# Both halves of the split activations side by side in one matmul: latents, attention gate and the first output projection of a two-layer trunk

## The chip, the cores and the metric

The kernel runs on one core of one Trainium2 chip. The core has a matrix engine (PE, TensorE, with a separate row PEld for its weight loads), a vector engine (DVE), a scalar engine (ACT) and an engine that issues transfers (SP). They work side by side and wait for each other by semaphores; each runs its own instructions in the order in which the program lists them. The metric is the device time of one execution in microseconds (us), smaller being better. A matmul's sums land in PSUM, a small memory in banks of 512 fp32 columns per partition, from which DVE and ACT read them.

## What is computed

Two layers over 256 tokens of width 2048, in float32. Cut to what matters here:

```python
def hybrid_layer(x, c_act, ...):
    mod = c_act @ w_mod + b_mod
    shift, scale, gate = jnp.split(mod, 3, axis=-1)
    h = rms_norm(x, g_norm) * (1.0 + scale[:, None, :]) + shift[:, None, :]
    proj = h @ w_in
    rq, rk, rv, rg, cq, ckv, kr, mg, bg = jnp.split(proj, points, axis=-1)
    ...                                            # retention branch: o_ret
    y_ret = (o_ret * jax.nn.silu(rg)) @ w_ret_proj
    q = (rms_norm(cq, g_cq) @ w_uq).reshape(B, S, MLA_HEADS, MLA_NOPE + MLA_ROPE)
    ...                                            # rotary part of q and of the shared key
    kv = (rms_norm(ckv, g_ckv) @ w_ukv).reshape(B, S, MLA_HEADS, MLA_NOPE + MLA_DV)
    o_mla = mla_attention(q_nope, q_rope, k_nope, k_rope, v)
    y_mla = (o_mla * jax.nn.silu(mg)) @ w_mla_proj
    g_a, g_b = jnp.split(jax.nn.sigmoid(bg), 2, axis=-1)
    merged = g_a * y_ret + g_b * y_mla
    return x + gate[:, None, :] * (merged @ w_out)
```

`cq` and `ckv` (512 columns each) are the latents, `mg` (2048 columns, 128 for each of 16 heads) is the attention gate, `w_out` is the output projection.

## The kernel before, in words

**Split products.** Every large product is made of three fp32r matmuls. A float32 weight block of 1024 columns per partition is loaded by SP into a buffer `wst` (5 of them), ACT copies its rounded upper part, DVE subtracts to get the rest (`split_into`, L239 to L241), both into one buffer `whl` (3 of them, so a split waits until PE is done with the block three before it). Activations are kept split in the same way by the class `Pairs`: one tile of 1024 columns holds, for two blocks of 128 rows of the contraction, the upper parts (256 tokens each) and behind them the lower parts. A product is upper x upper + upper x lower + lower x upper.

**Which operand moves.** In `proj` (L283) the weights are the stationary operand and the 256 tokens move, so every matmul has 256 columns. `chunk` (L267) lists for one weight block first the two products of the upper weights, one after the other (L273), and then the one of the lower weights (L276); all three add into the same 256 columns of PSUM. Two output blocks of 128 rows share one tile `acc` of 512 columns. In `proj_tok` the activations are stationary and 512 columns of weights move.

**PSUM.** There are four tiles `acc` and four tiles `aux`. A new `acc` tile takes the buffer that comes free first in the order that the scheduler plans, and the first matmul into it waits for the last reader of its predecessor.

**Order.** The kernel is written as one long program; the Tile framework's scheduler plans it with a timeline and writes the order of each engine's instructions. `tc.high_priority()` lets some go ahead of what stands before them. So a change in a few lines can move instructions elsewhere.

**Places that the change touches.** `latent` (L657) makes the normalised latents of a layer by one `proj` of 512 columns (two `acc` tiles), squares and a row norm. The attention loop (L792) goes over 8 pairs of heads in each layer. One turn: products with `w_uq` into two `acc` tiles (`acc<-c,whl`: `a1`, whose readers are ACT's copy `qn` L818 and the split `q1`, and `a2`, whose reader is the rotation, four short DVE products L481 and one L482); products with `w_ukv` into two more (`a1` read by ACT's copy `kn` L836 and the split `k1`, `a2` by ACT's copy `vv` L838); scores (L846 on), softmax; the gate's product (`acc<-h,whl`, four weight blocks) into one `acc` tile, Silu (L873); transposes of the weights of attention (L880) and their copies `p` and `pT` (L882); the product with v (`aux<-p,v`, and `aux<-mg,vv` L887, which reads `pT`); times the gate (L889, DVE); split into `z`. PE works on one turn's gate while the next turn's `w_uq` and `w_ukv` products are close behind. Layer 0's output projection (L915) goes through 16 blocks of `w_out` and adds each, scaled, to `xT` (L921). Layer 1's output projection is another function and stays.

Of the kernel before, what the change touches and what calls it, by code (L numbers as in the profile page):

```python
# [13 lines left out]
AF = mybir.ActivationFunctionType  # L14
ALU = mybir.AluOpType
AX = mybir.AxisListType

P = 128
S = 256
D = 2048  # L20
KT = D // P
# [6 lines left out]
RANK = 512  # L28
# [10 lines left out]
C_MG = C_KR + ROPE  # L39
# [69 lines left out]
def trunk(ctx: ExitStack, tc: tile.TileContext, x, c, positions, w_mod, b_mod, g_norm, w_in, g_cq,  # L109
# [14 lines left out]
    def acc_tile():  # L124
        return pacc.tile([P, 2, S], F32, name="acc", tag="acc")
# [4 lines left out]
    def tmp_tile():  # L130
        return tp.tile([P, 512], F32, name="tmp", tag="tmp")
# [15 lines left out]
    class Pairs:  # L147
# [13 lines left out]
        def block(self, kt, cols=slice(None)):  # L161
            return [u[:, kt % 2, cols] for u in self.pair(kt // 2)]

    cst = cp.tile([P, K_COLS], F32, name="cst")
    DMA.dma_start(cst, consts)
    ident = cst[:, K_ID : K_ID + P]
# [34 lines left out]
    xT = cp.tile([P, KT, S], F32, name="xT")  # L201
# [47 lines left out]
    def load_split(src, nk, n, early=False):  # L249
        if prepared and not early:  # L250
            return prepared.pop(0)
        bg()
        w = load(src, nk, n)
        t = hp.tile([P, 2, 1024], F32R, name="whl", tag="whl")
        hi = t[:, 0, : nk * n].rearrange("p (k n) -> p k n", k=nk)
        lo = t[:, 1, : nk * n].rearrange("p (k n) -> p k n", k=nk)
        with tc.high_priority(offset=SPLITS):
            last_split.append(split_into(hi, lo, w))
        return hi, lo
# [18 lines left out]
    def proj_chunk(accs, hi, lo, k0, nk, span, act):  # L278

        chunk([(accs[j // 2][:, j % 2, :], (hi[:, k, j * P : (j + 1) * P], lo[:, k, j * P : (j + 1) * P]),  # L280
                act.block(k0 + k), k0 + k == span[0] and j % 2 == 0, k0 + k == span[1] - 1, False)
               for k in range(nk) for j in range(hi.shape[2] // P)])

    def proj(w, col, n, act, span=(0, KT)):
        accs = [acc_tile() for _ in range((n + 2 * P - 1) // (2 * P))]
        nk = 1024 // n
        for k0 in range(*span, nk):
            hi, lo = load_split(w[k0 * P : (k0 + nk) * P, col : col + n], nk, n)
            proj_chunk(accs, hi, lo, k0, nk, span, act)
        return accs  # L290

    def proj_tok(w, col, act, span=(0, KT)):
# [163 lines left out]
    def add_squares(sq, pair):  # L456

        src = xT[:, 2 * pair : 2 * pair + 2, :]
        if pair in (0, KT // 2 - 1):
            sq.append(dp.tile([P, 2, S], F32, name="sq", tag="dtab"))  # L460
            A.activation(sq[-1], src, AF.Square)
        else:
            t = tmp_tile().rearrange("p (a b) -> p a b", a=2)
            A.activation(t, src, AF.Square)
            V.tensor_tensor(sq[0], sq[0], t, ALU.add)
# [158 lines left out]
    def layer(l, r, u):  # L624
# [31 lines left out]

        def latent(col, g):  # L657
            dst = Pairs("c")
            accs = proj(W, col, RANK, hh)
            raw = tmp_tile(), tmp_tile()  # L660
            s2 = tmp_tile()
            t = tmp_tile()
            with tc.high_priority():
                for a in range(2):
                    fa = accs[a].rearrange("p a b -> p (a b)")
                    A.activation(raw[a], fa, AF.Copy)
                    A.activation((s2, t)[a], fa, AF.Square)
                V.tensor_tensor(s2, s2, t, ALU.add)
                rr = rstd_rows([s2.rearrange("p (a b) -> p a b", a=2)], RANK)
                for k in range(4):  # L670
                    rk_ = raw[k // 2][:, (k % 2) * S : (k % 2 + 1) * S]
                    V.scalar_tensor_tensor(rk_, rk_, g[:, k : k + 1], rr, ALU.mult, ALU.mult)
                for a in range(2):
                    split_into(*dst.flat(a), raw[a])
            return dst
# [112 lines left out]
        for g in range(MH // 2):  # L788
# [80 lines left out]
            p1 = two(t1, 0, S), two(t1, 512, S)  # L869
            t1 = quarter("v1", F32R)  # L870
            v1 = t1[:, 0:256], t1[:, 256:512]
            accs = proj(W, C_MG + g * 256, 256, hh)
            A.activation(mg, accs[0], AF.Silu)  # L873

            split_into(*v1, vv[:, 0, :])
            po = aux_tile()
# [35 lines left out]
            last_output(w_out[l], mm)  # L912
            return None, None
        sq = []
        for f0, nf in ((0, 4), (4, 4), (8, 4), (12, 2), (14, 2)):  # L915
            accs = proj(w_out[l], f0 * P, nf * P, mm)
            with tc.high_priority() if f0 == 14 else nullcontext():
                for a, acc in enumerate(accs):
                    for b in range(2):
                        f = f0 + 2 * a + b  # L920
                        V.scalar_tensor_tensor(xT[:, f, :], acc[:, b, :], mods[l][:, 32 + f : 33 + f], xT[:, f, :],  # L921
                                               ALU.mult, ALU.add)
                    add_squares(sq, f0 // 2 + a)
                if f0 == 0:
                    A.activation(small(1), sq[0][:, 0, 0:1], AF.Sqrt)
                if f0 == 14:
                    r = spread(rstd_cols(sq, D), dp.tile([P, S], F32, name="r1", tag="dtab"))
            if f0 == 8:
                left(0)
                n = GROUPS[l + 1][0][1]  # L930
                make_amul(l + 1, 0, n)
                u = scaled(l + 1, n)
# [96 lines left out]
```

## Time and profile before

| | |
|---|---|
| median of 3 runs | 2056.74 us (2056.7 to 2057.08) |
| the profiled execution, its own time | 2057.32 us |
| its span from first to last instruction | 2055.5 us |
| PE busy | 2025.8 us, 99%, 12414 recorded matmuls |
| DVE, ACT busy | 1483.6 us (72%), 1061.7 us (52%) |
| DMA | 460.59 MB, 224 GB/s over the span |
| granted clock of PE | 0.997 of full speed |

Busy time of PE counts a matmul until its result is out; matmuls overlap, so the distance from the start of one group to the start of the next is the better measure of what they cost. A timeline row gives the start, the time until the end, engine, line, operation, output and inputs (buffer numbers left out; the moving input is named first), partitions x columns and, as x16, how many instructions were merged; in square brackets the engine's idle time before it and what ended it. An fp32 matmul of `aux<-mg,vv` or `aux<-qkn` is recorded twice, an fp32r one once.

### The profile page before, as it was taken

To read this page: it belongs to the slowest core of one execution; us is meant where nothing else is said; L and a number is where in the kernel's file an instruction comes from. 1 tells how busy PE (TensorE), PEld (TensorE's weight loads), DVE (VectorE), ACT (ScalarE), POOL (GpSimd) and SP (SyncE) were. 2 spreads that over 40 slices of the span, in tenths; PEclk is the share of its full clock that TensorE was granted. 3 is DMA by queue.
4 is the path that set the end of the run, shared out by engine and by line. 5 is a ranking of instruction groups with operands and counts; after the bars stand their busy time and mean duration, and the time that the engine had idled before them with its cause. 6 is when DMAs were issued, how large, how long until landed. Compare 5 with 4: busy or idle time off the path is not lost.

```text
span 2055.5 us, 31773 instructions
## 1 busy us (share of the span) xinstructions
PE 2025.8 (99%) x12414; PEld 1802.8 (88%) x12414; DVE 1483.6 (72%) x2082; ACT 1061.7 (52%) x1489; POOL 0.2 (0%) x4
## 2 busy tenths in 40 slices
PE   7999999999999999999999999999999999999998
PEld 4888888998899998889998888889889999988887
DVE  5799986778777777775577776568776877765574
ACT  4554355654456664444454464456544666644453
POOL 0000000000000000000000000000000000000000
PEclk9999999999999999999999999999999999999999
DMA  8998966567866668875569966665677666666572
GB/s 315 321 310 274 308 198 194 159 191 259 302 191 195 195 187 274 281 267 185 182 196 333 326 209 189 194 180 156 198 238 223 205 185 195 208 224 192 190 243 90
DMA packets 251222, 460.59 MB, mean 224 GB/s; under 512 B 18464, under 2 KB 68032, under 8 KB 251072
## 3 DMA queue, kind: packets, MB, share of 16 engines
q1 hardware_dynamic: 251072, 458.57, 69.8%
q8 instruction: 97, 1.59, 0.3%
q14 instruction: 53, 0.43, 0.1%
HBM read 456.41 MB, written 2.10 MB: 223 GB/s over the span
## 4 chain that ended last, share of the span: by engine, by line
PE 94%; DMA 3%; DVE 2%; ACT 1%; issue 1%; SPq 0%; ACTq 0%; DVEq 0%
PE acc L273 57%; PE acc L276 28%; DMA ring<-in_w_mod 2%; DMA wmod<-in_w_mod 1%; PE aux L264 1%; PE aux L265 1%; PE aux L263 1%; PE acc L263 1%; PE acc L264 1%; PE acc L265 1%; DVE extra L349 0%; PE aux L880 0%; ACT whl L240 0%; PE aux L721 0%; PE aux L846 0%
## 5 line engine op out<-in xcount | busy, mean ns | idle before, releaser
L240 ACT ACTIVATE whl<-wst 128x1024 fp32r<-128x1024 f32 (+1 forms) x708 | 709.0, 1007 | 805.0 <-PE acc L276 699.1
L241 DVE TENSOR_TENSOR whl<-wst,whl 128x1024 fp32r<-128x1024 f32 (+1 forms) x708 | 814.2, 1156 | 378.3 <-ACT whl L240 374.3
L273 PE MATMUL acc<-whl,h 128*128 128x512 f32 x2048 | 515.4, 392 | 0.0
L273 PEld LDWEIGHTS acc<-whl,h 128*128 128x128 f32 x2048 | 381.4, 188 | 77.1
L273 PE MATMUL acc<-h,whl 128*128 128x256 f32 x2432 | 328.1, 285 | 4.0 <-ACT h L240 2.4
L273 PEld LDWEIGHTS acc<-h,whl 128*128 128x128 f32 x2432 | 307.8, 192 | 6.3 <-ACT h L240 3.2
L276 PE MATMUL acc<-whl,h 128*128 128x512 f32 x1024 | 279.6, 392 | 0.4 <-DVE whl L241 0.4
L273 PE MATMUL acc<-whl,z 128*128 128x512 f32 x1024 | 254.8, 390 | 1.2 <-ACT whl L240 1.2
L273 PEld LDWEIGHTS acc<-whl,z 128*128 128x128 f32 x1024 | 191.8, 188 | 41.1 <-ACT whl L240 1.6
L276 PEld LDWEIGHTS acc<-whl,h 128*128 128x128 f32 x1024 | 190.9, 188 | 39.4 <-DVE whl L241 1.0
L276 PE MATMUL acc<-h,whl 128*128 128x256 f32 x1216 | 176.3, 284 | 0.0
L276 PEld LDWEIGHTS acc<-h,whl 128*128 128x128 f32 x1216 | 158.7, 192 | 0.1
L276 PE MATMUL acc<-whl,z 128*128 128x512 f32 x512 | 137.1, 390 | 0.0
L400 DVE SCALAR_TENSOR_TENSOR macc<-ring,cact,macc 128x1024 f32<-128x1024 f32 x75 | 96.1, 1281 | 35.7 <-DMA ring<-in_w_mod 35.2
L400 DVE SCALAR_TENSOR_TENSOR macc<-wst,cact,macc 128x1024 f32<-128x1024 f32 x90 | 115.0, 1278 | 0.0
L276 PEld LDWEIGHTS acc<-whl,z 128*128 128x128 f32 x512 | 96.0, 188 | 20.1 <-DVE whl L241 0.2
L273 PE MATMUL acc<-c,whl 128*128 128x256 f32 x640 | 100.2, 288 | 0.0
L273 PEld LDWEIGHTS acc<-c,whl 128*128 128x128 f32 x640 | 85.9, 191 | 0.2
L273 PE MATMUL acc<-m,whl 128*128 128x256 f32 x512 | 67.3, 283 | 0.0
L273 PEld LDWEIGHTS acc<-m,whl 128*128 128x128 f32 x512 | 64.0, 192 | 0.1
L276 PE MATMUL acc<-c,whl 128*128 128x256 f32 x320 | 57.6, 285 | 0.0
L273 PE MATMUL acc<-whl,m 128*128 128x512 f32 (+1 forms) x256 | 56.5, 365 | 0.0
(256 smaller groups left out, 1880.1 us busy)
## 6 DMA issues: line engine op xcount, KB each, us to landing
wst<-in_w_in SPq DMA_DIRECT2D x416, 512.0 KB, 4.4
wst<-in_w_mod SPq DMA_DIRECT2D x96, 512.0 KB, 4.7
ring<-in_w_mod SPq DMA_DIRECT2D x80, 512.0 KB, 5.3
wst<-in_w_ret_proj SPq DMA_DIRECT2D x64, 512.0 KB, 4.8
wst<-in_w_mla_proj SPq DMA_DIRECT2D x64, 512.0 KB, 4.4
wst<-in_w_out SPq DMA_DIRECT2D x64, 512.0 KB, 3.7
wst<-in_w_ukv SPq DMA_DIRECT2D x32, 512.0 KB, 4.3
wst<-in_w_uq SPq DMA_DIRECT2D x32, 384.0 KB, 4.2
```

The costliest lines, as they stand in the source:

```text
L240: A.activation(hi, src, AF.Copy)
L241: return V.tensor_tensor(lo, src, hi.bitcast(F32), ALU.subtract)
L263: T.matmul(o, a[0], b[0], start=start, stop=False, skip_group_check=True)
L264: T.matmul(o, a[0], b[1], start=False, stop=False, skip_group_check=True)
L265: T.matmul(o, a[1], b[0], start=False, stop=stop, skip_group_check=True)
L273: T.matmul(o, x, y, start=start and i == 0, stop=False, skip_group_check=True)
L276: T.matmul(o, x, y, start=False, stop=stop, skip_group_check=True)
L400: V.scalar_tensor_tensor(macc, w, cact[:, k : k + 1], macc, ALU.mult, ALU.add)
```

## The change

A new method `both` returns, for one block of the contraction, upper and lower activations side by side: 128 x 2 x 256, the two runs 512 columns apart. A new function `proj_sum` makes 256 output columns with two `acc` tiles, one for each output block of 128 rows: the upper weights multiply both parts in one matmul of 512 columns (the two halves of the tile get the two products), the lower weights multiply the upper part into the second half. The sum of the two halves is made afterwards: by ACT's copy and a DVE addition (latents, gate), or by two additions into `xT` (output projection of layer 0). Weight blocks are 4 x 256 columns in all three places.

```diff
+        def both(self, kt):
+            self.pair(kt // 2)
+            return self.tiles[kt // 2][:, :, kt % 2, :]
...
+    def proj_sum(w, col, act):
+        accs = [acc_tile() for _ in range(2)]
+        for k0 in range(0, KT, 4):
+            hi, lo = load_split(w[k0 * P : (k0 + 4) * P, col : col + 256], 4, 256)
+            todo = [(accs[j], k0 + k, (hi[:, k, j * P : (j + 1) * P], lo[:, k, j * P : (j + 1) * P]))
+                    for k in range(4) for j in range(2)]
+            for o, kt, u in todo:
+                T.matmul(o, u[0], act.both(kt), start=kt == 0, stop=False, skip_group_check=True)
+            for o, kt, u in todo:
+                T.matmul(o[:, 1, :], u[1], act.block(kt)[0], start=False, stop=kt == KT - 1, skip_group_check=True)
         return accs
...
         def latent(col, g):
-            accs = proj(W, col, RANK, hh)
+            accs = proj_sum(W, col, hh), proj_sum(W, col + 256, hh)
...
                 for a in range(2):
-                    fa = accs[a].rearrange("p a b -> p (a b)")
-                    A.activation(raw[a], fa, AF.Copy)
-                    A.activation((s2, t)[a], fa, AF.Square)
+                    for b, acc in enumerate(accs[a]):
+                        bs = slice(b * S, (b + 1) * S)
+                        A.activation(raw[a][:, bs], acc[:, 0, :], AF.Copy)
+                        V.tensor_tensor(raw[a][:, bs], raw[a][:, bs], acc[:, 1, :], ALU.add)
+                    A.activation((s2, t)[a], raw[a], AF.Square)
...
-            accs = proj(W, C_MG + g * 256, 256, hh)
-            A.activation(mg, accs[0], AF.Silu)
+            for b, acc in enumerate(proj_sum(W, C_MG + g * 256, hh)):
+                A.activation(mg[:, b, :], acc[:, 0, :], AF.Copy)
+                V.tensor_tensor(mg[:, b, :], mg[:, b, :], acc[:, 1, :], ALU.add)
+            A.activation(mg, mg, AF.Silu)
...
-        for f0, nf in ((0, 4), (4, 4), (8, 4), (12, 2), (14, 2)):
-            accs = proj(w_out[l], f0 * P, nf * P, mm)
-            with tc.high_priority() if f0 == 14 else nullcontext():
-                for a, acc in enumerate(accs):
-                    for b in range(2):
-                        f = f0 + 2 * a + b
-                        V.scalar_tensor_tensor(xT[:, f, :], acc[:, b, :], mods[l][:, 32 + f : 33 + f], xT[:, f, :],
+        for f0 in range(0, KT, 2):
+            accs = proj_sum(w_out[l], f0 * P, mm)
+            with tc.high_priority() if f0 == KT - 2 else nullcontext():
+                for b, acc in enumerate(accs):
+                    f = f0 + b
+                    for part in range(2):
+                        V.scalar_tensor_tensor(xT[:, f, :], acc[:, part, :], mods[l][:, 32 + f : 33 + f], xT[:, f, :],
                                                ALU.mult, ALU.add)
```

The scheduler makes a new order from it. The first place is PE in the attention loop of layer 0, between the second turn's last product with v (L887) and the third turn's first score (L846, `aux<-qkn`) and first gate matmul (`acc<-h,whl`). Before, with what each instruction waits for in brackets, three matmuls after that product with v:

```order
L276 MATMUL acc<-c,whl 128x256 x2
L276 MATMUL acc<-whl,c 128x256 x2
L273 MATMUL acc<-c,whl 128x256 x4
L273 MATMUL acc<-whl,c 128x256 x4
L273 MATMUL acc<-c,whl 128x256 x4
L273 MATMUL acc<-whl,c 128x256 x4
L276 MATMUL acc<-c,whl 128x256 [waits DVE_49]
L276 MATMUL acc<-c,whl 128x256
L276 MATMUL acc<-whl,c 128x256 x2
L276 MATMUL acc<-c,whl 128x256 x2
L276 MATMUL acc<-whl,c 128x256 x2
L273 MATMUL acc<-h,whl 128x256 [waits DVE_49,Activation_49]
```

The same place of the changed kernel (its L909 is L887 of before, L866 is L846, L305 is the new matmul of 512 columns, L278 and L281 are L273 and L276):

```order
L909 MATMUL aux<-mg,vv 128x128 [waits Activation_49]
L278 MATMUL acc<-whl,c 128x256 x7
L281 MATMUL acc<-c,whl 128x256 [waits DVE_49]
L281 MATMUL acc<-c,whl 128x256
L281 MATMUL acc<-whl,c 128x256 x2
L281 MATMUL acc<-c,whl 128x256 x2
L281 MATMUL acc<-whl,c 128x256 x2
L866 MATMUL aux<-qkn 128x128 [waits Activation_49]
L866 MATMUL aux<-qkn 128x128 [waits PE_49]
L305 MATMUL acc<-h,whl 128x512 [waits PE_49,Activation_49]
```

Fifteen matmuls stand now between the last product with v and the scores, where 31 stood before the gate's first matmul and 22 of the gate's own before the scores; and the gate's first matmul waits for ACT (the copy `vv`), where it waited for DVE (the rotation's L482).

The second place is ACT in the same turn. Before, from the table load of the gate's Silu (L873) to the copy `kn` (L836) of the next turn:

```order
L873 ACT_TABLE_LOAD
L873 ACTIVATE mg<-acc 128x512
L240 ACTIVATE v_5201<-vv 128x256
L240 ACTIVATE p_5200<-aux 128x256 x2
L240 ACTIVATE whl<-wst 128x1024
L882 ACTIVATE mg<-aux 128x128 x2
L240 ACTIVATE whl<-wst 128x1024 x2
L240 ACTIVATE z<-tmp 128x512
L818 ACTIVATE qkn<-acc 128x256
L240 ACTIVATE q_5354<-acc 128x256
L836 ACTIVATE qkn<-acc 128x256
```

The changed kernel's second turn (L893 is the new copy, L895 the Silu, L904 the copies `pT`, L856 the copy `kn`):

```order
L893 ACTIVATE mg<-acc 128x256
L245 ACTIVATE p_5389<-aux 128x256 x2
L245 ACTIVATE whl<-wst 128x1024 x2
L895 ACT_TABLE_LOAD
L895 ACTIVATE mg<-mg 128x512
L904 ACTIVATE mg<-aux 128x128 x2
L245 ACTIVATE whl<-wst 128x1024
L245 ACTIVATE z<-tmp 128x512
L838 ACTIVATE qkn<-acc 128x256
L245 ACTIVATE q_5516<-acc 128x256
L856 ACTIVATE qkn<-acc 128x256
```

The Silu and its table load have moved from ahead of the copies `p` to behind them and behind two weight splits, directly ahead of `pT`, which the last product with v reads.

## Rows read from the trace of the kernel before

**Rows 1.** The page, part 4: the chain that ended last, by engine, then by line.
```profile
PE 94%; DMA 3%; DVE 2%; ACT 1%; issue 1%; SPq 0%; ACTq 0%; DVEq 0%
```

**Rows 2.** Windows; stretch, length, busy PE PEld DVE ACT POOL, clock, DMA share, GB/s.
```profile
387.00:447.00 60.00, 60.00 (x479) 59.18 (x479) 49.97 (x104) 33.71 (x50) 0.00 (x0) 1.00 0.51 148
565.80:771.00 205.20, 204.94 (x1734) 204.52 (x1733) 158.94 (x303) 131.92 (x258) 0.00 (x0) 1.00 0.64 192
952.70:1046.50 93.80, 93.80 (x785) 93.80 (x784) 57.02 (x82) 42.46 (x51) 0.00 (x0) 1.00 0.57 180
```

**Rows 3.** Timeline of PE, 320 to 340 us: one weight block with 512 moving columns.
```profile
320.92 1.98 PE L273 MATMUL acc<-whl,h 128*128 128x512 f32 x8
322.73 1.07 PE L276 MATMUL acc<-whl,h 128*128 128x512 f32 x4
323.64 1.98 PE L273 MATMUL acc<-whl,h 128*128 128x512 f32 x8
```

**Rows 4.** Timeline of all engines, 622.6 to 630.5 us: from one turn to the next.
```profile
623.40 0.38 PE L887 MATMUL aux<-mg,vv 128*128 128x128 f32 x2
623.82 0.69 DVE L889 TENSOR_TENSOR tmp<-aux,mg 128x512 f32<-128x512 f32 x1 [0.72 <-PE aux L887]
624.54 1.72 DVE L481 TENSOR_TENSOR tmp<-acc,sin_t 32x256 f32<-32x256 f32 x4
625.66 0.62 ACT L240 ACTIVATE z<-tmp 128x512 fp32r<-128x512 f32 x1
625.88 0.64 PE L273 MATMUL acc<-whl,c 128*128 128x256 f32 x4
626.18 0.37 ACT L818 ACTIVATE qkn<-acc 128x256 f32<-128x256 f32 x1
626.27 0.42 DVE L482 TENSOR_TENSOR qkn<-acc,cos_t 128x256 f32<-128x256 f32 x1
626.36 0.40 PE L276 MATMUL acc<-c,whl 128*128 128x256 f32 x2
626.44 0.38 ACT L240 ACTIVATE q<-acc 128x256 fp32r<-128x256 f32 x1
627.28 0.39 ACT L836 ACTIVATE qkn<-acc 128x256 f32<-128x256 f32 x1 [0.46 <-PE acc L276]
627.32 2.08 PE L273 MATMUL acc<-h,whl 128*128 128x256 f32 x16
628.99 0.60 ACT L838 ACTIVATE vv<-acc 128x512 f32<-128x512 f32 x1
629.24 0.88 PE L276 MATMUL acc<-h,whl 128*128 128x256 f32 x6
629.96 0.61 PE L846 MATMUL aux<-qkn 128*128 128x128 f32 x4
630.33 0.36 PE L276 MATMUL acc<-h,whl 128*128 128x256 f32 x1
```

**Rows 5.** Timeline of all engines, 674 to 679.6 us: the gate's first matmul late.
```profile
678.52 0.40 PE L276 MATMUL acc<-whl,c 128*128 128x256 f32 x2
678.61 0.42 DVE L482 TENSOR_TENSOR qkn<-acc,cos_t 128x256 f32<-128x256 f32 x1
679.18 0.59 PE L273 MATMUL acc<-h,whl 128*128 128x256 f32 x3 [0.26 <-DVE qkn L482]
```

**Rows 6.** Timeline of all engines, 596.6 to 601.7 us: another turn's gate product.
```profile
596.97 0.38 PE L887 MATMUL aux<-mg,vv 128*128 128x128 f32 x2
598.50 0.68 DVE L889 TENSOR_TENSOR tmp<-aux,mg 128x512 f32<-128x512 f32 x1
```

**Rows 7.** Lines by form on DVE, 952.7 to 1046.5 us: additions into xT.
```profile
L921 DVE SCALAR_TENSOR_TENSOR xT<-acc,mod,xT 128x256 f32<-128x256 f32 x14 | 5.8, 476 | 1.0 <-PE acc L276 1.0
```

**Rows 8.** Timeline of all engines, 1043 to 1053.5 us: the end of layer 0.
```profile
1047.73 0.61 ACT L461 ACTIVATE sq<-xT 128x512 f32<-128x512 f32 x1
1049.88 0.95 PE L319 MATMUL aux<-ones,sq 128*128 128x1 f32 x8
```

More of the change, by code (lines that the diff above doesn't have):

```diff
@@ L289, in proj @@
             proj_chunk(accs, hi, lo, k0, nk, span, act)
+        return accs
+    def proj_sum(w, col, act):
[8 more added lines that the diff above has]
+                T.matmul(o[:, 1, :], u[1], act.block(kt)[0], start=False, stop=kt == KT - 1, skip_group_check=True)
         return accs
@@ L914, in layer @@
         sq = []
-        for f0, nf in ((0, 4), (4, 4), (8, 4), (12, 2), (14, 2)):
-            accs = proj(w_out[l], f0 * P, nf * P, mm)
-            with tc.high_priority() if f0 == 14 else nullcontext():
-                for a, acc in enumerate(accs):
-                    for b in range(2):
-                        f = f0 + 2 * a + b
-                        V.scalar_tensor_tensor(xT[:, f, :], acc[:, b, :], mods[l][:, 32 + f : 33 + f], xT[:, f, :],
+        for f0 in range(0, KT, 2):
[5 more added lines that the diff above has]
+                        V.scalar_tensor_tensor(xT[:, f, :], acc[:, part, :], mods[l][:, 32 + f : 33 + f], xT[:, f, :],
                                                ALU.mult, ALU.add)
-                    add_squares(sq, f0 // 2 + a)
+                add_squares(sq, f0 // 2)
                 if f0 == 0:
                     A.activation(small(1), sq[0][:, 0, 0:1], AF.Sqrt)
-                if f0 == 14:
+                if f0 == KT - 2:
                     r = spread(rstd_cols(sq, D), dp.tile([P, S], F32, name="r1", tag="dtab"))
-            if f0 == 8:
+            if f0 == 10:
                 left(0)
```

## The prediction, made before the changed kernel ran

> **What bounds the kernel now.** I read the chain of waits first: PE holds 94% of the chain that ended last [rows 1], so the question at every edit is what it does to PE's stream. Then the windows of the three places that the change touches: PE is busy for all of a latents stretch, for 204.94 of 205.20 us of layer 0's attention loop and for all of its output projection [rows 2]. There is no slack on PE to be filled; a change can only make its stream shorter or open gaps in it. In the same windows DVE is busy for 158.94 of 205.20 us (77%) and ACT for 131.92 (64%) of the attention loop, so both have room in the mean; whether they have it at the moment when PE needs them is read from the timeline. The granted clock is 1.00 in all three, so a matmul has one price.
>
> **What PE saves.** Start to start, 12 matmuls of 512 columns take 323.64 - 320.92 = 2.72 us, 226.7 ns each [rows 3]. Sixteen of 256 columns take 629.24 - 627.32 = 1.92 us, 120 ns each [rows 4]. Twice the columns cost 106.7 ns more, so each matmul has 13.3 ns besides its columns. A trio of products is now 3 x 120 = 360 ns, with the change 226.7 + 120 = 346.7. A moving operand in two runs is no dearer: the `acc<-whl,c` matmuls move 2 x 128 columns from two places and take (626.36 - 625.88)/4 = 120 ns [rows 4]. Upper-weight matmuls replaced by half as many: two layers x (8 turns x 2 output blocks + 8 output blocks of latents) x 16 contraction blocks = 512 + 256, and 16 x 16 = 256 for `w_out` in layer 0. That is 1024 matmuls fewer, 1024 x 13.3 ns = **-13.65 us**. Columns and bytes of weights stay.
>
> The Trainium skill, page "TensorE: Matmul & The Clock Gate", section "Back-to-back issue gap", speaks against this. Its warm spacing of a single matmul is N/2.4 + 2.5 ns, by which a merged pair saves an estimated 2.5 ns and the whole change 2.6 us. The rows above disagree with it: 120 and 226.7 ns where it has 109 and 216.
>
> **What is added beside PE.** Latents: 16 copies of 256 columns more on ACT and 16 additions on DVE, at about 0.38 and 0.42 us as `q` and L482 have it [rows 4]; ACT is busy for 33.71 and DVE for 49.97 of 60.00 us [rows 2]; the four DVE additions per latent fit into what is free. The output projection: 16 more additions into `xT` at 476 ns [rows 7] = 7.6 us on a DVE that is busy for 57.02 of 93.80 [rows 2]. At the end of layer 0 two more of them (0.95 us) stand before the last squares; the squares end at 1048.34 and PE asks for them at 1049.88 [rows 8], so 1.54 us cover it. Weight blocks of 4 x 256 columns carry the same bytes at a DMA share of 0.51 to 0.57. I take 0 for all of these; if that cover were gone, the last term would cost at most 0.95 us.
>
> **What the attention loop loses.** The gate's product now needs two `acc` tiles where it had one, six a turn over four buffers. So its first matmul stands close behind the readers of the `w_uq` and `w_ukv` tiles: the rotation L482 (`cos`) or the copy `vv`. And the Silu, now behind a copy and an addition, stands on ACT behind `p` and two weight splits, directly ahead of `pT`; the last product with v reads `pT`, so the scheduler puts that product later in PE's order. Both shorten the same stretch: before, 31 to 37 matmuls of `w_uq` and `w_ukv` lie between it and the gate's first matmul; the changed order has 15 to 19 there in ten of the fourteen turns behind the first of each layer, and 32 or more in the rest.
>
> How late the gate then is, with t = 0 at the start of the last row of L887, 623.40 [rows 4]. PE: 31 matmuls took 627.32 - 623.40 = 3.92 us, 31 x 0.12 and 0.20 for the product with v itself; so after 15, 16 or 19 it stands at 2.00, 2.12 or 2.48. DVE: L889 begins at 0.42, then come the four products of the rotation, and `cos` ends at 626.69, at 3.29. PE follows its end by 679.18 - 679.03 = 0.15 [rows 5], so the gate can begin at 3.44. ACT: `z` can start when L889 has ended, 1.18 with a like lag; `qn` starts 0.52 after `z`, the next two 0.26 each, so `kn` starts at 2.22 and ends at 2.61; `vv` ended 629.59 - 627.28 = 2.31 after the start of `kn`, so here at 4.53, and the gate that waits for it begins at 4.68. Scores that stand ahead of the gate take 630.33 - 629.96 = 0.37 us of a wait [rows 4]. From the changed order, by turn:
> two turns with 15 matmuls and no scores ahead, for `cos`: 2 x (3.44 - 2.00) = 2.9 us;
> one with 15 and scores: 3.44 - 2.37 = 1.1;
> three with 19 and scores: 3 x (3.44 - 2.85) = 1.8;
> three for `vv`, one with 15 and two with 16 and scores: (4.68 - 2.37) + 2 x (4.68 - 2.49) = 6.7;
> one with 15, scores, and a DVE addition of 128x512 (0.69 us, as L889) ahead of `cos`: 1.07 + 0.69 = 1.8.
> Together **+14.2 us**. In before, every turn waits for `cos` too, but 31 matmuls cover it.
>
> Two smaller terms. In three turns DVE's changed order has L889 behind a weight subtraction and an addition. Such a turn of before begins L889 at 598.50 - 596.97 = 1.53 instead of 0.42 [rows 6], 1.11 late; whether the subtraction waits for its block is not to be read from before, so the bounds are 0 and 3.3, and as these two starts are all that the rows have, I take some 0.4 each, **+1.3**. And before's one gap of this kind, where PE would have gone on at 678.52 + 2 x 0.12 and began at 679.18 [rows 5], goes: **-0.4**.
>
> The new copies (0.38) and additions (0.42) of the gate add 0.85 us to each turn of DVE; outside the moments above they lie in the 23% that DVE is free, and cost nothing.
>
> **The sum.** -13.65 + 14.2 + 1.3 - 0.4 = +1.4 us on the profiled execution's 2057.3, 2058.8. The median of the runs is 0.6 below that execution: **2058.2 us**. The kernel gains its 13.65 us in all three places (6.8 of them in the gate) and gives all back at the gate.
>
> The bounds of the waits: 0, when L889 and the copies come as early as PE; and all ten turns 1.11 later still, as in [rows 6], +11.1. Without waits the time is 2056.74 - 13.65 = 2043; with all of them 2069.
>
> **The rivals.**
> Faster: the waits are half of what I count, or less. For it: the last product with v waits for `pT` itself, and where that makes PE late, the weight splits and rotation of the next turn have gone on meanwhile and `cos` is nearer; and DVE is free for 23% of the loop [rows 2]. Against: L889 is behind that product in any case, and the rotation is behind L889 on DVE. At half the waits it gives 2058.2 - 7 = 2051, at none 2043; I put it at 2050. Chance 0.26.
> Slower: the 77% of DVE is not spread evenly, and six accumulators over four buffers make DVE's order the bound: in each of the ten short turns L889 begins 1.53 behind the product with v, as in [rows 6], because a weight subtraction or the new addition stands ahead of it. Each 0.1 us of such lateness costs 1.0 us over ten turns, so from about 0.35 us a turn the kernel is slower beyond doubt; at 1.11 it takes 2058.2 + 11.1 - 1.3 = 2068. For it: L889 is late in [rows 6] with less on DVE than now. Against: in [rows 4] it is not. I put it at 2066. Chance 0.27.
> The change doesn't do what it says: a matmul of 512 columns with the activations moving in two runs of 256 takes as long as two of 256, and nothing is saved. For it nothing in the rows; against it [rows 3, 4]. By the order, waits come all the same: 2056.7 + 15.1 = about 2072; with the page's 2.5 ns per pair about 2069. Chance 0.03.
> Weight blocks of 4 x 256 arrive later than those of 2 x 512 and PE waits for splits: at a DMA share of 0.57 [rows 2] I see no reason; 5 us, 2063. Chance 0.02.
>
> **How the numbers follow.** The forecast has 0.42, by itself from 2053.5 to 2061 (a third of the waits less, or the late L889 in five turns). With the parts of the faster and the slower case that lie next to it the range is 2048 to 2068, which leaves out 0.1 below (waits of less than a third) and 0.1 above. A measurement tells 0.2% from no change, 4.1 us: 2052.6 to 2060.9 is "same". The forecast puts 0.36 there, 0.05 above, 0.01 below; the faster case 0.25 below, 0.01 same; the rest, 0.32, is slower. Faster 0.26, same 0.37, slower 0.37.
>
> **What would show it.** Gate, latents and output projection of layer 0 with PE starts 227 ns apart for 512 columns and 120 for 256; the output projection stretch at about 90.4 instead of 93.80 us and each latents stretch 1.7 us shorter, both without waits; the attention loops no shorter than 205 us although their matmuls are 3.4 us shorter, with waits of PE ahead of the gate's first matmul, for DVE's `cos` in seven turns and ACT's `vv` in three, of 0.6 to 2.3 us each and 10 to 15 us in all. Wrong I would be if these waits sum to less than 7 us or more than 20, if they stand elsewhere (ahead of the product with v, or of the matmuls of a split block), or if the 512-column matmuls are not 227 ns apart.

## The result and the profile after

The changed kernel takes 2077.01 us (median of 5 runs, 2072.71 to 2078.41) where the kernel before took 2057.08 beside it: a ratio of 1.0092, 95% interval 1.0081 to 1.0102. It is slower by 19 to 20 us, outside the predicted range of 2048 to 2068. The profiled execution took 2077.47 us, 20.15 more than that of before (2057.32).

The chain that ended last, by engine, answers to [rows 1]: PE has lost 3 points of it.

```profile
PE 91%; DVE 3%; ACT 2%; DMA 2%; issue 1%; SPq 0%; ACTq 0%; DVEq 0%
```

To see where, I counted the columns of each kind of matmul and took the same matmul in both traces. The changed kernel is 2.6 us behind by 372 us, 3.9 behind at 524 (after the latents of layer 0), 12.6 behind at 796 (after its attention), 9.7 behind at 1058 (after its output projection), 11.0 behind at 1575 (latents of layer 1), 19.7 behind at 1805, and stays there. So, with differences taken before rounding, the two attention loops cost 8.7 us each, the stretches with the latents 1.2 to 1.3 each, the output projection gains 2.8, and 2.6 us are lost before any changed line.

Windows (stretch, length, busy PE PEld DVE ACT POOL, clock, DMA share, GB/s) of layer 0's attention and output projection, which answer to [rows 2]:

```profile
569.70:783.90 214.20, 204.86 (x1481) 191.67 (x1480) 162.23 (x314) 135.81 (x272) 0.00 (x0) 1.00 0.61 182
965.20:1056.20 91.00, 91.00 (x528) 80.22 (x527) 62.36 (x96) 43.35 (x51) 0.00 (x0) 1.00 0.60 186
```

From the first `w_uq` matmul to the last gate matmul the loop took 205.43 us before and takes 214.17 now, and PE is idle for 9.3 us of it, where [rows 2] had 0.26. The waits of PE in the whole changed kernel (engine and line, what it waited for: idle us, times, longest), only those that before had not or had smaller:

```profile
PE acc L305 <- DVE qkn L500: 6.4, 5, 2.2
PE aux L866 <- ACT qkn L856: 5.8, 8, 1.2
PE acc L278 <- ACT whl L245: 3.8, 4, 1.2
PE acc L305 <- ACT vv L858: 3.6, 3, 1.2
PE acc L305 <- DVE tmp L500: 1.8, 2, 0.9
PE acc L305 <- ACT k L245: 0.8, 1, 0.8
```

The gate's first matmul (L305) waits for the rotation (`qkn` L500) and for `vv` (L858): the places that the prediction named. In eight turns the scores (L866) that stand ahead of the gate wait first, for `kn` (L856); the prediction had those scores only as 0.37 us that fill a wait. The others (L278 for weight splits, `tmp` L500) stand in and behind the latents, and it had nothing there. A new merged block, from the timeline of PE in the latents (start, us to the end, line, operation), answers to [rows 3, 4]:

```profile
402.69 2.00 PE L305 MATMUL acc<-h,whl 128*128 128x512 f32 x8
404.52 1.11 PE L307 MATMUL acc<-h,whl 128*128 128x256 f32 x8
405.48 2.00 PE L305 MATMUL acc<-h,whl 128*128 128x512 f32 x8
```

Eight trios take 405.48 - 402.69 = 2.79 us, 349 ns each, where the prediction had 346.7 and before 360: a merged matmul takes 229 ns, not 226.7. At the end of layer 0 the last squares end at 1058.76, 0.91 us ahead of the matmul that reads them. In [rows 8] they ended 1.54 ahead, so the change used 0.63 us of that cover, where the prediction allowed for 0.95:

```profile
1058.13 0.63 ACT L479 ACTIVATE sq<-xT 128x512 f32<-128x512 f32 x1 [0.51 <-DVE xT L943]
1059.67 0.95 PE L337 MATMUL aux<-ones,sq 128*128 128x1 f32 x8
```

**One turn as predicted.** All engines at the place of [rows 4] in layer 0, from the second turn to the third, with L909 for L887, L911 for L889, L856 for L836 and L858 for L838:

```profile
629.41 0.38 PE L909 MATMUL aux<-mg,vv 128*128 128x128 f32 x2
629.83 0.69 DVE L911 TENSOR_TENSOR tmp<-aux,mg 128x512 f32<-128x512 f32 x1 [2.15 <-PE aux L909]
630.55 0.63 ACT L245 ACTIVATE z<-tmp 128x512 fp32r<-128x512 f32 x1 [0.54 <-DVE tmp L911]
631.62 0.39 ACT L856 ACTIVATE qkn<-acc 128x256 f32<-128x256 f32 x1
632.06 0.71 PE L866 MATMUL aux<-qkn 128*128 128x128 f32 x4 [0.48 <-ACT qkn L856]
633.31 0.62 ACT L858 ACTIVATE vv<-acc 128x512 f32<-128x512 f32 x1
633.98 0.74 PE L305 MATMUL acc<-h,whl 128*128 128x512 f32 x2 [1.21 <-ACT vv L858]
```

With t = 0 at 629.41: L911 at 0.42, `kn` at 2.21 to 2.60, `vv` to 4.52, the gate at 4.57. The prediction had 0.42, 2.22 to 2.61, 4.53 and 4.68.

**The next turn, not as predicted.**

```profile
657.04 0.38 PE L909 MATMUL aux<-mg,vv 128*128 128x128 f32 x2
657.32 1.23 DVE L246 TENSOR_TENSOR whl<-wst,whl 128x1024 fp32r<-128x1024 f32 x1 [1.21 <-ACT whl L245]
658.46 0.68 DVE L911 TENSOR_TENSOR tmp<-aux,mg 128x512 f32<-128x512 f32 x1
660.91 0.42 DVE L500 TENSOR_TENSOR qkn<-acc,cos_t 128x256 f32<-128x256 f32 x1
661.39 0.96 PE L305 MATMUL acc<-h,whl 128*128 128x512 f32 x3 [2.18 <-DVE qkn L500]
```

A weight subtraction (L246), which waited for its block, began 0.28 us into the turn and held DVE until 658.46. L911 begins 1.42 us behind the product with v instead of 0.42, the rotation ends at 661.33, and the gate begins at 4.35 instead of 3.44.

### The profile page after: what moved, and what is told of

Same layout as the page of the kernel before. It is cut to its first block, busy times and chain, and to the rows that moved or that the text cites. A ratio compares the mean times of both kernels' runs of the same rounds, so it can differ in the third digit from the quotient of the medians.

```text
span 2075.3 us, 29849 instructions
## 1 busy us (share of the span) xinstructions
PE 2025.0 (98%) x11390; PEld 1752.8 (84%) x11390; DVE 1503.4 (72%) x2146; ACT 1074.0 (52%) x1529; POOL 0.2 (0%) x4
## 4 chain that ended last, share of the span: by engine, by line
PE 91%; DVE 3%; ACT 2%; DMA 2%; issue 1%; SPq 0%; ACTq 0%; DVEq 0%
PE acc L278 44%; PE acc L281 22%; PE acc L305 11%; PE acc L307 6%; DMA ring<-in_w_mod 1%; ACT whl L245 1%; DMA wmod<-in_w_mod 1%; PE aux L268 1%; PE aux L270 1%; PE aux L269 1%; PE acc L269 1%; PE acc L268 1%; PE acc L270 1%; DVE tmp L499 0%; DVE whl L246 0%
## 5 line engine op out<-in xcount | busy, mean ns | idle before, releaser
L246 DVE TENSOR_TENSOR whl<-wst,whl 128x1024 fp32r<-128x1024 f32 (+1 forms) x708 | 813.9, 1156 | 385.5 <-ACT whl L245 382.0
L278 PE MATMUL acc<-whl,h 128*128 128x512 f32 x2048 | 514.1, 391 | 0.0
L278 PEld LDWEIGHTS acc<-whl,h 128*128 128x128 f32 x2048 | 381.7, 188 | 77.5
L281 PE MATMUL acc<-whl,h 128*128 128x512 f32 x1024 | 279.9, 393 | 0.4 <-DVE whl L246 0.4
L278 PE MATMUL acc<-whl,z 128*128 128x512 f32 x1024 | 255.0, 390 | 3.8 <-ACT whl L245 3.8
L278 PEld LDWEIGHTS acc<-whl,z 128*128 128x128 f32 x1024 | 191.6, 188 | 45.1 <-ACT whl L245 5.6
L281 PEld LDWEIGHTS acc<-whl,h 128*128 128x128 f32 x1024 | 190.6, 188 | 39.1 <-DVE whl L246 1.2
L305 PE MATMUL acc<-h,whl 128*128 128x512 f32 x768 | 205.6, 399 | 12.6 <-DVE qkn L500 6.4
L305 PEld LDWEIGHTS acc<-h,whl 128*128 128x128 f32 x768 | 135.7, 189 | 37.1 <-DVE qkn L500 6.4
L281 PE MATMUL acc<-whl,z 128*128 128x512 f32 x512 | 137.7, 390 | 0.0
L278 PE MATMUL acc<-h,whl 128*128 128x256 f32 x896 | 120.5, 288 | 3.8 <-ACT h L245 2.5
L278 PEld LDWEIGHTS acc<-h,whl 128*128 128x128 f32 x896 | 114.6, 196 | 5.2 <-ACT h L245 3.2
L307 PEld LDWEIGHTS acc<-h,whl 128*128 128x128 f32 x768 | 110.3, 191 | 10.1
L307 PE MATMUL acc<-h,whl 128*128 128x256 f32 x768 | 115.5, 284 | 0.0
L281 PEld LDWEIGHTS acc<-whl,z 128*128 128x128 f32 x512 | 95.7, 188 | 19.9 <-DVE whl L246 0.2
L278 PE MATMUL acc<-c,whl 128*128 128x256 f32 x640 | 97.9, 287 | 0.0
L278 PEld LDWEIGHTS acc<-c,whl 128*128 128x128 f32 x640 | 85.7, 191 | 0.4
L305 PE MATMUL acc<-m,whl 128*128 128x512 f32 x256 | 64.3, 392 | 0.0
L281 PE MATMUL acc<-h,whl 128*128 128x256 f32 x448 | 64.2, 287 | 0.0
```

What stands on the lines that cost most here:

```text
L246: return V.tensor_tensor(lo, src, hi.bitcast(F32), ALU.subtract)
L278: T.matmul(o, x, y, start=start and i == 0, stop=False, skip_group_check=True)
L281: T.matmul(o, x, y, start=False, stop=stop, skip_group_check=True)
L305: T.matmul(o, u[0], act.both(kt), start=kt == 0, stop=False, skip_group_check=True)
L307: T.matmul(o[:, 1, :], u[1], act.block(kt)[0], start=False, stop=kt == KT - 1, skip_group_check=True)
```

## The experiments

**One part alone.** Three kernels, each with one of the three places changed and the other two as before.

> Only layer 0's output projection uses the new function; latents and gate stay as before. Theory (the loss lies in the attention loop and, smaller, behind the latents; each part adds up by itself): the output projection's stretch gets 2.8 us shorter, as in the changed kernel, nothing else moves: 0.998 to 0.999 of the kernel before, about 2054.3 us. Rival (the matmuls of 512 columns are no gain as such, and what the changed kernel gains here comes from work that was moved): no change, 1.000.

> Only the attention gate uses the new function. Theory (six accumulators a turn over four buffers, and the Silu placed behind p, make PE wait about 20 us in 14 turns; the merged matmuls give back 4.7 us in the gate): both attention loops together 16 to 18 us longer than before, the kernel at 2072 to 2075 us, 1.0075 to 1.009. Rival (the late start of the product times the gate on DVE, which makes the waits longer than predicted, comes from the latents and the other parts' instructions moved into the loop): waits of only 14 us, the loops 8 us longer, about 2065 us.

> Only the latents use the new function. Theory (in each layer a wait of about 1.2 us for an accumulator and one or two of 1.2 us for a weight split eat the 1.2 us that the merged matmuls give): 1 to 3 us slower than before, 2058 to 2060 us, 1.0005 to 1.0015. Rival (those waits were made by the gate's code, which pulls the order of the whole layer, and the latents alone gain): 2.4 us faster, 2054.5 us.

Measured, each against the kernel before at 2056.99 us: output projection alone 2054.13 us, 0.9988 (0.9979 to 0.9996); gate alone 2076.09, 1.0093 (1.0079 to 1.0106); latents alone 2060.28, 1.0015 (1.0006 to 1.0024). The theory's numbers, but for 1 us more in the gate and 0.3 in the latents. -2.9 + 19.1 + 3.3 = 19.5 us: the parts add up, and the gate is the loss. Its waits in the attention loops are, line by line, those of the changed kernel (6.4 for the rotation, 5.8 at the scores, 3.6 for `vv`), so they don't come from the other parts.

**Upper and lower part in one run.** The layout of a pair, with every other line and PE's order the same:

```diff
-                self.tiles[i] = quarter(self.name, F32R).rearrange("p (s a b) -> p s a b", s=2, a=2)
+                self.tiles[i] = quarter(self.name, F32R).rearrange("p (a s b) -> p s a b", s=2, a=2)
```

> The changed kernel with one difference: in every pair of split activations the upper and the lower part of a block lie directly behind each other, so that the moving operand of a merged matmul is one run of 512 columns instead of two runs of 256; PE's order of instructions is the same. In the changed kernel a merged matmul takes 231 ns from start to start, where one with 512 weight columns moving takes 227. Theory A (the two runs cost the 4 ns): 227 ns, 1024 x 4 = 4 us faster than the changed kernel, about 2073 us. Theory B (the 4 ns have another cause): 231 ns as before, about 2077 us, or slower where ACT and DVE now write in two runs.

2076.3 us, 1.0088 (1.0074 to 1.0102): no gain that can be told from the changed kernel's 2077.01. Theory A falls. The same block as above, from the timeline of PE:

```profile
400.46 2.00 PE L307 MATMUL acc<-h,whl 128*128 128x512 f32 x8
402.30 1.11 PE L309 MATMUL acc<-h,whl 128*128 128x256 f32 x8
403.25 2.00 PE L307 MATMUL acc<-h,whl 128*128 128x512 f32 x8
```

Eight trios take 2.79 us as before. What makes 229 ns of 227 stays open; two runs of 256 cost nothing against one of 512.

**Two accumulators, matmuls not merged.** The gate alone, with

```diff
-                T.matmul(o, u[0], act.both(kt), start=kt == 0, stop=False, skip_group_check=True)
+                T.matmul(o[:, 0, :], u[0], act.block(kt)[0], start=kt == 0, stop=False, skip_group_check=True)
+                T.matmul(o[:, 1, :], u[0], act.block(kt)[1], start=False, stop=False, skip_group_check=True)
```

> Only the gate is changed, with its two accumulators, copies, additions and Silu as in the changed kernel, but each merged matmul of 512 columns is taken apart again into two of 256 columns. Theory (two accumulators and their readers make the waits, whatever the matmuls look like): nothing is saved and the waits stay; the order has seven of the fourteen later turns with 16 to 19 matmuls ahead of the scores and the gate, instead of ten, which by the sums of the prediction is 10 us, with the late starts on DVE 12 to 16: 2069 to 2073 us. Rival (the merged matmuls make the waits, since PE comes to the gate sooner with them): no waits, 2057 us.

2076.29 us, 1.0087 (1.007 to 1.0104). The rival falls: there are no merged matmuls, and the waits of the gate are there (3.7 us for the rotation, 3.6 for `vv`, 3.6 at the scores, 1.4 for `k`). The theory's size was too small, 2073 at most: like the prediction, it counted too little for late starts on DVE.

**Silu earlier.** The gate alone, its two copies, additions and Silu inside `with tc.high_priority():`.

> Only the gate is changed, and its copies, additions and Silu are put ahead of what stands before them (high priority), so that the Silu no longer stands between p and pT on ACT in most turns. The order then has three short turns with 22 matmuls and four or five with 15 to 19. Theory (the place of the Silu sets how late the product with v is put, and so how much of the next turn covers the gate's wait): waits 6 us less than with the gate alone, 2068 to 2071 us. Rival (the waits come from DVE, where the product times the gate starts late behind splits and the work for the modulation; the Silu's place is of no account): 2075 us or more.

2072.69 us, 1.0071 (1.0056 to 1.0086), 3.4 less than the gate alone. The loops are 1.7 and 2.9 us shorter; 1.5 of the 2.9 is a fall of the clock (last section) that layer 1 had with the gate alone and has not here. So the place of the Silu is a part of the cause and a small one: some 3 us of 20.

**Five accumulators.** The gate alone, and the kernel before as its control, both with

```diff
-    pacc = ctx.enter_context(tc.tile_pool(name="pacc", bufs=4, space=bass.MemoryType.PSUM))
-    paux = ctx.enter_context(tc.tile_pool(name="paux", bufs=4, space=bass.MemoryType.PSUM))
+    pacc = ctx.enter_context(tc.tile_pool(name="pacc", bufs=5, space=bass.MemoryType.PSUM))
+    paux = ctx.enter_context(tc.tile_pool(name="paux", bufs=3, space=bass.MemoryType.PSUM))
```

> Only the gate is changed, with five accumulator buffers and three of the other kind instead of four and four. The gate's first matmul then waits neither for the rotation nor for the copy vv. Theory (the accumulator that the gate takes over from the rotation or from vv is where the time goes): the waits of 20 us go but for some 3, the 5.8 us that the merged matmuls save remain: 2051 to 2057 us. Rival (DVE and ACT are late anyway, the wait moves to the product with v or to the scores): 2065 us or more.

> The kernel before with five accumulator buffers and three of the other kind, no other edit: the control for the run with the gate. Theory: 2056 to 2058 us, since PE waits for the accumulators of the kernel before for only 0.4 us in the attention loops. Rival (three buffers of the other kind make scores and transposes wait): 2060 us or more.

Gate 2057.2 us, 0.9997 (0.9988 to 1.0006); control 2060.98, 1.0014 (1.0004 to 1.0023). With a fifth accumulator the gate is 3.8 us faster than its control instead of 19 slower; the waits of PE for `qkn`, `vv` and `k` in the two loops shrink from 16.6 us idle to 0.8:

```profile
PE aux L864 <- ACT qkn L854: 0.5, 1, 0.5
PE acc L305 <- DVE qkn L500: 0.3, 1, 0.3
```

The control is 3.6 us slower than before, as its rival had it in size but not in place: its loops take 204.76 and 205.16 us, no more than before. Its profiled execution loses 2.3 us ahead of 372 us, 1.3 of them where the clock fell as it did in the changed kernel (last section), then 1.1 and 2.0 us in the stretches ahead of the two loops, where the gate with five accumulators loses 1.1 and 1.4 too; why stays open.

**The modulation's work out of the loops.** DVE also adds up the next modulation (`macc`, 1.28 us each), woven into the loop by a rate. The gate alone, and the kernel before as its control, both with

```diff
-        rate[0] = (RM, BG1)[l]
+        rate[0] = 0.0
```

> Only the gate is changed, and the products for the next modulation (additions of 128x1024 into macc on DVE, 1.28 us each, with their transfers) are not woven into the attention loops but come behind them. The order then has 33 matmuls between the product with v and the gate in each of the fourteen later turns, though the gate still has two accumulators. It is read from the attention loops, since what is put off costs elsewhere. Theory (six accumulators over four buffers do harm because DVE's extra work makes the products with v late; without it the cover of before is back): the waits of 21 us in the loops fall to 0 to 11 us (0.8 us in a turn in which L911 starts late), the loops take 0 to 11 us less than with the gate alone plus 2 us, at most 410 us in all. Rival (the two accumulators alone make the waits): the loops stay at 18 us above before.

> The kernel before with the modulation's additions put behind the attention loops, no other edit: the control for the run with the gate alone and the same edit (0.9971). Theory (these additions do harm only together with six accumulators a turn): 2056 to 2059 us, since PE waits only 0.4 us in the loops of before. Rival (putting them off is a gain by itself, and the gate's merged matmuls still lose): 2052 us.

Gate 2052.11 us, 0.9971 (0.996 to 0.9983); control 2057.15, 0.9998 (0.9989 to 1.0007). The gate has its two accumulators, its copies and additions, and wins 5 us. Layer 0's loop has no wait at all (window: PE busy for all of it, DVE for 144.94 of 201.20), and all fourteen later turns look like this one (all engines; L907 and L909 are L909 and L911 of the changed kernel):

```profile
565.40:766.60 201.20, 201.20 (x1457) 190.19 (x1456) 144.94 (x295) 133.66 (x268) 0.00 (x0) 1.00 0.57 161
```

```profile
622.10 0.38 PE L907 MATMUL aux<-mg,vv 128*128 128x128 f32 x2
622.84 0.68 DVE L909 TENSOR_TENSOR tmp<-aux,mg 128x512 f32<-128x512 f32 x1
625.29 0.42 DVE L500 TENSOR_TENSOR qkn<-acc,cos_t 128x256 f32<-128x256 f32 x1
626.26 1.09 PE L305 MATMUL acc<-h,whl 128*128 128x512 f32 x4
```

The rotation ends at 625.71, 33 matmuls keep PE busy until 626.26, and the 0.55 us between them are slack. The edit does two things at once: L909 begins 0.75 us behind the product with v in every turn, and the order has 33 matmuls of cover in all of them. These runs don't tell the two apart. The loops of the control take 203.84 and 203.83 us, those of the gate 201.13 and 201.16: 2.7 us each for 256 merged pairs.

**The rotary key apart.** The latents alone, the key's product in an `aux` buffer:

```diff
-            acc = acc_tile()
+            acc = aux_tile().rearrange("p (a b) -> p a b", a=2)
```

> Only the latents are changed, as in the run with the latents alone, and the product for the rotary key, which is made between them, gets a buffer of the other kind, so that no latent takes over an accumulator from the key's rotation. Theory (in each layer the wait of 1.2 us for the rotation goes, the wait for weight splits behind it stays): 2.4 us less than with the latents alone, 2057 to 2058.5 us. Rival (the wait moves to the splits or the order changes more than that): 2060 us.

2061.35 us, 1.0017 (1.0008 to 1.0025): no gain, the theory falls and its rival is right. The waits of PE around the latents of layer 0, of the changed kernel and then of this one:

```profile
PE acc L278 <- ACT whl L245: 2.3, 2, 1.2
PE acc L305 <- DVE tmp L500: 0.9, 1, 0.9
```

```profile
PE acc L305 <- ACT whl L245: 1.9, 2, 1.6
PE acc L278 <- ACT whl L245: 1.2, 1, 1.2
PE acc L307 <- DVE whl L246: 0.3, 1, 0.3
```

With the latents alone the waits are those of the changed kernel. The wait for the rotation went and one for a weight split came: the order put ACT's copies of a latent ahead of the split that PE asks for next.

**Versions faster than both.** Gate and output projection changed, latents as before. First with a2 of the `w_ukv` products in an `aux` buffer, so that five accumulators a turn remain; then the same with the latents and the key's move too; then with the modulation put off instead; then with both remedies.

```diff
-            a1, a2 = acc_tile(), acc_tile()
+            a1, a2 = acc_tile(), aux_tile().rearrange("p (a b) -> p a b", a=2)
```

> Gate and output projection of layer 0 are changed, latents as before; in the attention loop the accumulator a2 of the w_ukv products (read by the copy vv) is a buffer of the other kind, so that five accumulators a turn stand over the four buffers, as before, and the gate waits for neither the rotation nor vv in most turns. Theory (the accumulators make the waits): waits of 0 to 4 us, saving 5.8 in the gate and 2.9 in the output projection: 2048.5 to 2053 us, faster than both kernels. Rival (with one more user of the other four buffers, scores and transposes wait): 2056 us or more.

> All three parts as in the changed kernel, with both moves of buffers: a2 of the w_ukv products and the rotary key's product get a buffer of the other kind. Theory (the parts add up): the run with gate and output projection plus what the latents do with the key apart, 2049 to 2054 us. Rival: the latents' own loss stays, 2 to 3 us above the run with gate and output projection.

> Gate and output projection of layer 0 changed, latents as before, the modulation's additions put behind the attention loops; no buffer is moved. Theory (parts add up): the run with the gate and the same edit (0.9971) less the 2.9 us of the output projection: 2049 us, 0.9957. Rival (the additions that are put off now meet the output projection's own additions on DVE): 2052 us or more.

> Gate and output projection of layer 0 changed, with both remedies: a2 of the w_ukv products in a buffer of the other kind, and the modulation's additions put behind the attention loops. Theory (two answers to one cause, each of which takes all of the waits away): no faster than either alone, 2048 to 2050 us. Rival (each takes away another part of the waits): 2045 us or less.

Measured: 2049.16 us, 0.9955 (0.9941 to 0.9968); with the latents 2051.51, 0.9969 (0.9958 to 0.9981); modulation put off 2048.39, 0.9957 (0.9944 to 0.9969); both 2048.36, 0.9955 (0.9941 to 0.9969). Theories as expected; in the second the time lies in the ranges of both theory and rival, and the latents cost 2.4 us. Either remedy takes the waits away and both together no more: one cause with two conditions, six accumulators over four buffers, and a DVE that has the modulation's additions as well, with the order that the scheduler makes of them. The kernel before was not run with a2 in an `aux` buffer, so this remedy has no control of its own. PE's window of layer 0's loop in the first, with DVE at 163.61 us, more than the changed kernel's 162.23, and no wait:

```profile
567.60:769.80 202.20, 202.20 (x1481) 190.90 (x1480) 163.61 (x313) 133.78 (x263) 0.00 (x0) 1.00 0.65 195
```

So it is not DVE's sum of work that makes PE wait, but whose readers the gate's accumulator stands behind. The third turn of that run shows it (PE and DVE; L907 and L909 as above):

```profile
626.26 0.38 PE L907 MATMUL aux<-mg,vv 128*128 128x128 f32 x2
628.38 1.09 PE L305 MATMUL acc<-h,whl 128*128 128x512 f32 x4
628.39 0.68 DVE L909 TENSOR_TENSOR tmp<-aux,mg 128x512 f32<-128x512 f32 x1
630.84 0.42 DVE L500 TENSOR_TENSOR qkn<-acc,cos_t 128x256 f32<-128x256 f32 x1
```

The order has 16 matmuls between the product with v and the gate, where the changed kernel has 15, and DVE begins its product 2.13 us behind. Still the gate begins without a wait, 2.88 us ahead of the rotation's end.

## Why the prediction was wrong

The mechanism in the attention loop was the one forecast: fewer matmuls, and the gate's first one late. Its sizes were not, and the main step that failed is "in three turns DVE's changed order has L889 behind a weight subtraction and an addition ... I take some 0.4 each, +1.3". By turn (the forecast of the ten short turns against the trace; waits from start to start, and when L911 began behind the last product with v, 0.42 being on time):

```
              layer 0, turns 2 to 8             layer 1, turns 2 to 8
forecast      0    2.31 1.44 1.76 0    0.59 2.19  0    0.59 0    2.19 1.44 1.07 0.59
measured      0.80 2.20 2.34 1.88 0.80 1.75 2.08  0    1.38 0.97 2.08 2.34 1.14 1.75
L911 begins   1.94 0.42 1.42 0.58 1.94 1.67 0.42  0.75 1.30 1.87 0.42 1.41 0.58 1.67
```

In the turns where L911 begins on time (0.42 or 0.58) the forecast is right to 0.12 us. In eight others it begins 1.30 to 1.94 behind, and the wait is 0.8 to 1.2 us longer than forecast. Measured are 21.5 us of waits, forecast 14.2, with the late starts 15.5. [Rows 6] had shown such a start, 1.53, and the slower rival took it for all ten turns; I gave it 0.27, and in the forecast three turns got 0.4 of its 1.11 us. Nor are two starts "all that the rows have" in the trace of before: L889 begins 0.42 us behind in five of its fourteen later turns and 0.91 to 1.53 in the other nine. So the late start was the common case already, hidden in all but one turn ([rows 5]) by the 37 matmuls of cover that each of those nine had. Three of the eight are turns with 31 or more matmuls of cover, which I had set to zero: 31 are not enough when L911 starts 1.9 late.

The rest of the 20.15 us, term by term, forecast +1.4:

- Merged matmuls, forecast -13.65. The output projection shrank from 93.76 to 91.03 us, 256 pairs at 10.7 ns, and the gate's loops in the runs without the modulation by 5.4 us, 512 pairs at 10.5 ns: **-10.9** for 1024. The fixed cost of [rows 3, 4], 13.3 ns, came from two different streams, one of weights and one of activations. The runs with a control decide: 10.5 ns. The Trainium skill ("TensorE: Matmul & The Clock Gate", "Back-to-back issue gap") has N/2.4 + 2.5 ns for a single warm matmul, from which a merged pair would save an estimated 2.5 ns; these runs disagree with it.
- Waits at the gate, forecast +15.5: **+21.5**, above. Before's own 0.4 went, as forecast.
- The latents, a second step that failed, forecast 0 beside their saving: each stretch lost 1.2 us although its 128 pairs save 1.4, **+5.2** for both layers. "The four DVE additions per latent fit into what is free" looked at the mean share of DVE. Here, too, four accumulators where there were two made PE wait for the key's rotation (0.9 us a layer), and PE waits longer for weight splits (3.8 us in all against 1.2 before). Taking one of these waits away showed only that another takes its place.
- Clock in layer 1's loop, not in the forecast: **+1.5**, below.
- Before the first changed line: **+2.6**. PE's order is the same there. In other kernels with the same start and the same buffers the stretch came out from 1.0 us faster than before (the control with the modulation put off) to 2.0 slower (gate unmerged). The run with upper and lower part side by side, which has the changed kernel's whole order, is 0.4 slower there. So this term belongs to the profiled execution and not to the change; 1.4 us of it stand where the clock fell (last section).

-10.9 + 21.5 - 0.4 + 5.2 + 1.5 + 2.6 = 19.5 of 20.15; the other 0.6 I have not placed. The waits alone, 6.0 us more than forecast, would have left the kernel at 2064, inside the range; with the latents' 5.2 it is 2069, outside. The sign of being wrong that I had named, waits of more than 20 us, came true.

What was right: that the 7.6 us of additions into `xT` cost nothing, as [rows 2, 7] allow (28 of them at 478 ns stand in a stretch with no wait); the layer boundary; weights in shorter runs. What decided is that the saving was priced from two different streams and the waits from one turn: the measured saving is 20% smaller, the measured waits are 40% larger, and a forecast that sets 14 against 15 left no room for either.

## What to carry to other kernels

Before merging two matmuls that then need two accumulators, count the accumulators per turn against the buffers, and name the reader that each first matmul will wait for: a 10 ns gain per pair was paid with up to 2 us per turn. Where such a reader stands in the order of an engine that also does unhurried work, price its lateness from every turn of the trace and not from the best one; either moving one accumulator to another pool or moving the unhurried work out of the loop turned the gate's 19 us of loss into some 5 of gain (the first was run with the output projection, whose 2.9 us are taken off). And a control with the same remedy on the kernel before (five accumulators: +3.6 us, modulation put off: none that can be told) is what tells the remedy from the cause.

## What the runs showed of the hardware that was not expected

A wait of PE can cost more than its length. In layer 1's loop, the fifth turn had two waits; behind them the granted clock fell. The timeline of PE:

```profile
1694.83 0.71 PE L866 MATMUL aux<-qkn 128*128 128x128 f32 x4 [0.36 <-ACT qkn L856]
1696.75 1.29 PE L305 MATMUL acc<-h,whl 128*128 128x512 f32 x4 [1.21 <-ACT vv L858]
1697.84 1.05 PE L307 MATMUL acc<-h,whl 128*128 128x256 f32 x4
1698.69 1.91 PE L305 MATMUL acc<-h,whl 128*128 128x512 f32 x4
1700.40 0.96 PE L307 MATMUL acc<-h,whl 128*128 128x256 f32 x4
1701.20 2.00 PE L305 MATMUL acc<-h,whl 128*128 128x512 f32 x8
```

Four matmuls of 512 columns took (1700.40 - 1698.69)/4 = 428 ns each, at the lower of its two levels (1.2 GHz), and the stretch from 1697.84 to 1701.20 lasted 3.36 us instead of 8 x 0.12 + 4 x 0.23 = 1.88. The third turn of layer 0, shown above, has nearly the same pair of waits, 0.48 and 1.21, and no fall. The run side by side, with PE's order the same, fell in both of these turns; the gate alone fell in both layers, unmerged and with the Silu earlier in layer 0 alone, and the kernels without waits in the loops in neither. The windows of the changed kernel, first a stretch ahead of every changed line, then this one; and of the kernel before, the first stretch again:

```profile
120.00:130.00 10.00, 8.30 (x50) 7.59 (x49) 6.90 (x8) 5.85 (x10) 0.00 (x0) 0.83 0.86 300
...
1695.00:1705.00 10.00, 8.79 (x41) 7.47 (x42) 6.30 (x12) 3.07 (x5) 0.00 (x0) 0.83 0.48 145
```

```profile
120.00:130.00 10.00, 8.31 (x62) 7.59 (x61) 8.20 (x9) 5.55 (x9) 0.00 (x0) 1.00 0.87 294
```

PE's order is the same in both first stretches, with the same two waits near 123 us (1.47 and 0.22 us in the kernel before, 1.47 and 0.23 in the changed one). The fourteen matmuls of 256 columns behind the second wait took 1.93 us in the kernel before and 2.97 in the changed one; 0.83 is the mean of a stretch that ran partly at the lower level. So whether a gap costs its length or some 1.5 us more can't be read from the order. That it is why the runs of the changed kernel spread over 5.7 us is a guess: one of them was profiled, and the kernel before, run beside the experiments, spread over up to 4.9 us too.
